# Order of one store, one load and eight residual adds around the second output group of a fused matmul, bias and residual kernel

## The chip, the cores and the metric

The kernel runs on one core of one Trainium2 chip. A core has a matrix engine (TensorE, called PE in the profile, with its weight loads as PEld), a vector engine (VectorE, DVE), a scalar engine (ScalarE, ACT), a general engine (GpSimd, POOL) and a queue processor (SyncE, SP) that here issues nearly all transfers between HBM and the on-chip memory. The transfers are carried out by 16 DMA engines. The metric is the device time of one execution in microseconds. "Before" is the kernel ahead of the change, "after" the kernel with it.

## The reference

```python
batch, m, k, n = 16, 512, 1024, 768
return (np.matmul(x, weight) + bias + residual).astype(np.float32)
```

All inputs and the output are float32. With the batch flattened there are 8192 rows: x is 8192 x 1024, the weight 1024 x 768, the bias has 768 numbers, residual and output are 8192 x 768. The page of the profile counts 61.88 MB read from HBM and 25.17 MB written.

## The kernel before, in words

The 8192 rows are worked on as 64 subtiles of 128 rows, t = 0 to 63, in 8 groups g of 8 subtiles (`G = 8`). A transfer moves a whole group: an x group is 4 MiB, a residual group 3 MiB, an output group 3 MiB. Only the first group of x and the weight are loaded in smaller pieces, and only the last output group is stored in pieces.

One subtile goes through the engines like this:

- `cast_x` (L121): ScalarE casts 128 x 1024 of x to bf16. There are five buffers for the result.
- `transpose` (L136): TensorE transposes it in eight 128 x 128 blocks into PSUM (two buffers).
- `copy_xt` (L143): VectorE copies the transposed block from PSUM to the on-chip memory (four buffers).
- `matmul` (L150): TensorE multiplies, 8 steps of k by 2 chunks of columns (512 and 256), into a PSUM tile of 128 x 768 (three buffers).
- `evacuate`: for groups 1 to 7, VectorE adds the PSUM tile to the residual tile, in place (L167), and GpSimd adds the bias, in place, afterwards (`add_bias`, L174). Group 0 is different: its residual isn't there yet, so VectorE adds bias to the PSUM tile and writes into a separate `o_tile` (L164), and the residual is added later, by GpSimd (`add_residual`, L178).

In the main loop, iteration t issues `cast_x(t + 3)`, the transposes of t + 1, the matmuls of t, `copy_xt(t + 1)` and `evacuate(t)`. Every instruction is recorded with `keep_in_program_order`, so each engine carries out its own instructions in the order in which the loop writes them. There is no scheduler. An engine whose next instruction has to wait holds everything behind it. This goes for the queue of SP too: a load that waits for a buffer holds the stores and loads written after it.

The residual groups, the staged weight and `o_tile` share four slots of 3 MiB, called ring0 to ring3. `HOME = [3, 1, 0, 3, 1, 2, 0, 3]` gives the slot of each residual group. Group 3's residual therefore goes where group 0's was: `load_r(3)` may not be issued until all eight `add_residual` have read group 0's residual. Group 4's goes where group 1's output was, so `load_r(4)` waits until `store(1)` has landed. Group 5's goes where `o_tile` was (`store(0)`). A store of a group waits for the bias adds of its eight subtiles.

The table `moves` gives the iterations at whose end SP's loads and stores are written. Around the change it says: the load of x group 3 and that of residual group 3 at t = 12, the store of group 1 at t = 15, the load of x group 4 at t = 20, the load of residual group 4 and the store of group 0 at t = 21, the load of x group 5 at t = 28. The eight residual adds are written at the end of t = 12, so on GpSimd they come ahead of the bias adds of subtiles 13, 14 and 15, for which `store(1)` waits.

At the end, the bias of subtiles 61 to 63 is added on VectorE ahead of time (t = 57 to 59), and group 7 is stored in five pieces of falling size, the last of which needs the last VectorE add (L293).

Of the kernel before, what the change touches and what calls it, by code (L numbers as in the profile page):

```python
# [11 lines left out]
G = 8  # L12
# [9 lines left out]
def kernel(  # L22
# [8 lines left out]
    nc = tc.nc  # L31
# [27 lines left out]
    def o(ins):  # L59
        return tc.keep_in_program_order(ins)  # L60
# [26 lines left out]
    x_tiles, r_tiles, o_tiles, w_stage = {}, {}, {}, {}  # L87
# [23 lines left out]
    def cast_x(t, split=False):  # L111
        if t >= n_sub:
            return
        xb_tiles[t] = slot(xb_pool, "xb", XB_BUFS, [P, K], BF16)
        src = x_tiles[t // G][:, t % G, :]
        if split:
            h = K // 2
            o(nc.scalar.copy(out=xb_tiles[t][:, :h], in_=src[:, :h]))  # L118
            o(nc.vector.tensor_copy(out=xb_tiles[t][:, h:], in_=src[:, h:]))  # L119
        else:  # L120
            o(nc.scalar.copy(out=xb_tiles[t], in_=src))  # L121
# [7 lines left out]
    def transpose(t):  # L129
        if t >= n_sub:  # L130
            return
        xb = xb_tiles.pop(t).rearrange("m (h p j) -> m h j p", p=P, j=4)
        pt = slot(pt_pool, "pt", PT_BUFS, [P, n_k, P], BF16)
        for k in range(n_k):
            h, j = divmod(k, 4)
            o(nc.tensor.transpose(out=pt[:, k, :], in_=xb[:, h, j, :], identity=ident))  # L136
        pt_tiles[t] = pt

    def copy_xt(t):
        if t >= n_sub:  # L140
            return
        xt_tiles[t] = slot(xt_pool, "xt", XT_BUFS, [P, n_k, P], BF16)
        o(nc.vector.tensor_copy(out=xt_tiles[t], in_=pt_tiles.pop(t)))  # L143

    def matmul(t, k0=0, k1=n_k):
        if t not in po_tiles:
            po_tiles[t] = slot(po_pool, "po", PO_BUFS, [P, N], FP32)
        for k in range(k0, k1):
            for (n0, nl) in chunks:
                o(nc.tensor.matmul(  # L150
                    po_tiles[t][:, n0:n0 + nl],
                    lhsT=xt_tiles[t][:, k, :],
                    rhs=w_sb[:, k, n0:n0 + nl],
                    start=(k == 0),
                    stop=(k == n_k - 1),
                ))

    def evacuate(t):


        g, j = divmod(t, G)
        po = po_tiles.pop(t)
        if g == 0:
            o(nc.vector.tensor_add(out=o_tiles[0][:, j, :], in0=po, in1=bias_bc))  # L164
        else:
            rt = r_tiles[g][:, j, :]
            o(nc.vector.tensor_add(out=rt, in0=po, in1=rt))  # L167
            if t < n_sub - 3:
                add_bias(t)
        xt_tiles.pop(t)  # L170

    def add_bias(t, engine=nc.gpsimd):
        rt = r_tiles[t // G][:, t % G, :]
        o(engine.tensor_add(out=rt, in0=rt, in1=bias_bc))  # L174

    def add_residual(t):
        ot = o_tiles[0][:, t, :]
        o(nc.gpsimd.tensor_add(out=ot, in0=ot, in1=r_tiles[0][:, t, :]))  # L178


    load_x(0, 0, 2)
# [42 lines left out]
    for k in range(2, 6):  # L224
# [19 lines left out]
    moves = {  # L244
        4: [(load_x, 2)],
        5: [(load_r, 0), (load_r, 2)],
        12: [(load_x, 3), (load_r, 3)],
        15: [(store, 1)],
        20: [(load_x, 4)],
        21: [(load_r, 4), (store, 0)],  # L250
        28: [(load_x, 5)],
# [11 lines left out]
    for t in range(3, n_sub - 1):  # L263
        cast_x(t + 3)
        if t == 3:
            matmul(t, 0, 5)
            transpose(t + 1)
            matmul(t, 5, 8)
        elif t == G - 1:
            matmul(t)  # L270
            transpose(t + 1)
        else:
            transpose(t + 1)
            matmul(t)
        copy_xt(t + 1)
        if n_sub - 7 <= t < n_sub - 4:
            add_bias(t + 4, nc.vector)
        evacuate(t)
        if t == 12:
            for u in range(G):  # L280
                add_residual(u)
        for move, *what in moves.get(t, []):
            move(*what)


    t = n_sub - 1
# [36 lines left out]
```

## Time and profile before

| what | value |
|---|---|
| median of 3 runs | 213.15 us (212.84 to 213.54) |
| profiled execution, device time | 214.12 us |
| its span in the profile | 212.3 us |
| mean granted TensorE clock | 0.993 |
| PE busy | 199.6 us (94%) |
| DVE busy | 110.3 us (52%) |
| POOL busy | 111.0 us (52%) |
| ACT busy | 66.7 us (31%) |
| queue q1 of the DMA engines | 87.03 MB, 97.3% of 16 engines' span |

The busy times are sums over the span. PE's are to be read with care: matmuls are pipelined and their ends are modelled, so that a busy PE is not PE at its peak. The span is cut into 40 slices of 5.3 us in the page's second part, with one digit for each engine and slice (tenths of busy time) and, for the DMA engines, their share and what they moved in GB/s. The timeline gives start and length of instructions; a number in brackets behind one is how long its engine sat idle ahead of it, and whom it waited for. For SP it gives the moments at which transfers are issued; the time to landing of each is told separately.

### The profile page before, as it was taken

To read this page: it belongs to the slowest core of one execution; us is meant where nothing else is said; L and a number is where in the kernel's file an instruction comes from. 1 tells how busy PE (TensorE), PEld (TensorE's weight loads), DVE (VectorE), ACT (ScalarE), POOL (GpSimd) and SP (SyncE) were. 2 spreads that over 40 slices of the span, in tenths; PEclk is the share of its full clock that TensorE was granted. 3 is DMA by queue.
4 is the path that set the end of the run, shared out by engine and by line. 5 is a ranking of instruction groups with operands and counts; after the bars stand their busy time and mean duration, and the time that the engine had idled before them with its cause. 6 is when DMAs were issued, how large, how long until landed. Compare 5 with 4: busy or idle time off the path is not lost.

```text
span 212.3 us, 3674 instructions
## 1 busy us (share of the span) xinstructions
PE 199.6 (94%) x1560; PEld 133.8 (63%) x1590; DVE 110.3 (52%) x143; ACT 66.7 (31%) x69; POOL 111.0 (52%) x68
## 2 busy tenths in 40 slices
PE   7797999999999999999999999999999999999960
PEld 7554666666666666666666666666666666666630
DVE  0646645545526554455445544554455445599630
ACT  2634409407330172200931046300751019300000
POOL 2000000366499999995566556555655665563600
PEclk9999999999999999999999999999999999999997
DMA  6999999999999899999999999999999999999993
GB/s 234 405 420 435 482 411 423 448 404 417 435 420 468 324 347 392 448 420 432 431 440 445 411 425 415 445 428 418 440 440 443 401 445 429 423 426 438 408 413 120
DMA packets 5640, 87.28 MB, mean 411 GB/s; under 512 B 628, under 2 KB 756, under 8 KB 2296
## 3 DMA queue, kind: packets, MB, share of 16 engines
q1 hardware_dynamic: 5616, 87.03, 97.3%
q8 instruction: 12, 0.20, 0.4%
q14 instruction: 4, 0.03, 0.0%
q10 hardware_dynamic: 8, 0.01, 0.0%
HBM read 61.88 MB, written 25.17 MB: 410 GB/s over the span
## 4 chain that ended last, share of the span: by engine, by line
PE 87%; DMA 7%; issue 1%; DVE 1%; ACT 0%; SPq 0%; POOL 0%; POOLq 0%
PE po L150 73%; PE pt L136 13%; DMA x_tile<-in_x_dram 4%; DMA bias_rows<-in_bias_dram 3%; PE last_ps L290 1%; DVE xt L143 1%; ACT xb L118 0%; DVE r_tile L293 0%; SPq L97 0%; POOL ident masks.py:197 0%; POOL bias_rows L73 0%; POOLq L307 0%
## 5 line engine op out<-in xcount | busy, mean ns | idle before, releaser
L150 PE MATMUL po<-w_sb,xt 128*128 128x512 bf16 (+1 forms) x978 | 172.2, 324 | 3.2 <-DVE xt L143 1.5
L174 POOL TENSOR_TENSOR r_tile<-r_tile,bias_bc 128x768 f32<-128x768 f32 x53 | 95.5, 1816 | 85.1 <-DVE r_tile L167 85.0
L150 PEld LDWEIGHTS <-xt 128*128 128x128 bf16 x1008 | 95.8, 98 | 59.7 <-DVE xt L143 2.5
L121 ACT CAST xb<-x_tile 128x1024 bf16<-128x1024 f32 x62 | 61.6, 1043 | 109.6 <-DMA x_tile<-in_x_dram 80.1
L167 DVE TENSOR_TENSOR r_tile<-po,r_tile 128x768 f32<-128x768 f32 x55 | 52.6, 956 | 76.1 <-PE po L150 65.8
L143 DVE COPY xt<-pt 128x1024 bf16<-128x1024 bf16 x64 | 43.5, 680 | 3.9 <-PE pt L136 3.9
L136 PEld LDWEIGHTS <-xb 128*128 128x128 bf16 x512 | 35.2, 113 | 9.3 <-ACT xb L118 2.0
L136 PE MATMUL pt<-ident,xb 128*128 128x128 bf16 x512 | 39.0, 219 | 1.4 <-ACT xb L118 1.4
L178 POOL TENSOR_TENSOR o_tile<-o_tile,r_tile 128x768 f32<-128x768 f32 x8 | 14.2, 1820 | 3.1 <-DMA r_tile<-in_residual_dram 3.1
L164 DVE TENSOR_TENSOR o_tile<-po,bias_bc 128x768 f32<-128x768 f32 x8 | 7.5, 952 | 4.8 <-PE po L150 4.8
L174 DVE TENSOR_TENSOR r_tile<-r_tile,bias_bc 128x768 f32<-128x768 f32 x3 | 6.6, 2188 | 0.0
L202 PE MATMUL warm_ps<-warm_in 128*128 128x128 bf16 x54 | 5.1, 275 | 1.1 <-DVE warm L76 1.1
L202 PEld LDWEIGHTS <-warm_in 128*128 128x128 bf16 x54 | 4.7, 129 | 1.0 <-DVE warm L76 1.0
L119 DVE CAST xb<-x_tile 128x512 bf16<-128x512 f32 x2 | 0.9, 426 | 6.3 <-DMA x_tile<-in_x_dram 6.3
L127 DVE CAST w_sb<-w_stage 128x768 bf16<-128x768 f32 x5 | 2.8, 558 | 2.5 <-DMA w_stage<-in_weight_dram 2.5
L125 ACT CAST w_sb<-w_stage 128x768 bf16<-128x768 f32 x3 | 2.5, 831 | 4.0 <-DMA w_stage<-in_weight_dram 4.0
L290 PE MATMUL last_ps<-w_sb,xt 128*128 128x512 bf16 (+1 forms) x16 | 2.8, 326 | 0.0
L290 PEld LDWEIGHTS <-xt 128*128 128x128 bf16 x16 | 1.6, 98 | 1.1
L118 ACT CAST xb<-x_tile 128x512 bf16<-128x512 f32 x2 | 1.2, 618 | 3.0 <-DMA x_tile<-in_x_dram 3.0
L77 ACT ACT_TABLE_LOAD x1 | 1.3, 1283 | 2.6 <-POOL ident masks.py:199 2.6
L293 DVE TENSOR_TENSOR r_tile<-last_ps,r_tile 128x512 f32<-128x512 f32 (+1 forms) x2 | 1.1, 558 | 1.0 <-PE last_ps L290 1.0
L228 DVE STREAM_SHUFFLE bias_bc<-bias_rows 128x768 f32<-128x768 f32 x1 | 1.0, 1012 | 0.0
(11 smaller groups left out, 2.1 us busy)
## 6 DMA issues: line engine op xcount, KB each, us to landing
x_tile<-in_x_dram SPq DMA_DIRECT2D x7, 4096.0 KB, 33.0
r_tile<-in_residual_dram SPq DMA_DIRECT2D x8, 3072.0 KB, 17.0
out_dram<-r_tile SPq DMA_DIRECT2D x6, 3072.0 KB, 23.9
x_tile<-in_x_dram SPq DMA_DIRECT2D x3, 1024.0 KB, 11.6
out_dram<-o_tile SPq DMA_DIRECT2D x1, 3072.0 KB, 23.9
w_stage<-in_weight_dram SPq DMA_DIRECT2D x6, 384.0 KB, 7.2
out_dram<-r_tile SPq DMA_DIRECT2D x1, 1536.0 KB, 9.7
x_tile<-in_x_dram SPq DMA_DIRECT2D x2, 512.0 KB, 7.9
```

Source lines behind the costliest of these rows:

```text
L121: o(nc.scalar.copy(out=xb_tiles[t], in_=src))
L125: o(nc.scalar.copy(out=w_sb[:, k, :], in_=w_stage[0][:, k, :]))
L127: o(nc.vector.tensor_copy(out=w_sb[:, k, :], in_=w_stage[0][:, k, :]))
L136: o(nc.tensor.transpose(out=pt[:, k, :], in_=xb[:, h, j, :], identity=ident))
L143: o(nc.vector.tensor_copy(out=xt_tiles[t], in_=pt_tiles.pop(t)))
L150: o(nc.tensor.matmul(po_tiles[t][:, n0:n0 + nl], lhsT=xt_tiles[t][:, k, :], rhs=w_sb[:, k, n0:n0 + nl], start=(k == 0), stop=(k == n_k - 1),))
L164: o(nc.vector.tensor_add(out=o_tiles[0][:, j, :], in0=po, in1=bias_bc))
L167: o(nc.vector.tensor_add(out=rt, in0=po, in1=rt))
L174: o(engine.tensor_add(out=rt, in0=rt, in1=bias_bc))
L178: o(nc.gpsimd.tensor_add(out=ot, in0=ot, in1=r_tiles[0][:, t, :]))
L202: o(nc.tensor.matmul(warm_ps, lhsT=warm_in, rhs=warm_in, start=True, stop=True))
L290: o(nc.tensor.matmul(ps, lhsT=xt_tiles[t][:, k, :], rhs=w_sb[:, k, n0:n0 + nl], start=(k == 0), stop=(k == n_k - 1)))
```

## The change

Three things are rearranged; no arithmetic is added or left out.

- On SP's queue, `load_r(3)` is moved from the end of t = 12 to the end of t = 17. `store(1)`, at t = 15, now stands ahead of it. Both stand between the load of x group 3 and that of x group 4, as before.
- On GpSimd, the residual adds are written at the end of t = 15 (`2 * G - 1`) in place of t = 12, behind the bias adds of all of group 1.
- Two of the eight residual adds, those of subtiles 0 and 1, go to VectorE, at t = 16 and t = 17, each between `copy_xt(t + 1)` and `evacuate(t)`. GpSimd keeps six.

```diff
-    def add_residual(t):
+    def add_residual(t, engine=nc.gpsimd):
         ot = o_tiles[0][:, t, :]
-        o(nc.gpsimd.tensor_add(out=ot, in0=ot, in1=r_tiles[0][:, t, :]))
+        o(engine.tensor_add(out=ot, in0=ot, in1=r_tiles[0][:, t, :]))
...
-        12: [(load_x, 3), (load_r, 3)],
+        12: [(load_x, 3)],
         15: [(store, 1)],
+        17: [(load_r, 3)],
         20: [(load_x, 4)],
...
             add_bias(t + 4, nc.vector)
+        if t in (2 * G, 2 * G + 1):
+            add_residual(t - 2 * G, nc.vector)
         evacuate(t)
-        if t == 12:
-            for u in range(G):
+        if t == 2 * G - 1:
+            for u in range(2, G):
                 add_residual(u)
```

## The prediction

> **What bounds the kernel now.** I read the page first: the slices, and the chain that ended last.
>
> ```profile
> PE   7797999999999999999999999999999999999960
> ...
> DMA  6999999999999899999999999999999999999993
> GB/s 234 405 420 435 482 411 423 448 404 417 435 420 468 324 347 392 448 420 432 431 440 445 411 425 415 445 428 418 440 440 443 401 445 429 423 426 438 408 413 120
> ...
> PE 87%; DMA 7%; issue 1%; DVE 1%; ACT 0%; SPq 0%; POOL 0%; POOLq 0%
> ```
>
> The chain says PE. But the DMA engines are just as full, and the only slices below 400 GB/s between the ramp and the end are the 14th to 16th (69 to 85 us). So two resources run neck and neck, and I ask which one ends last. The windows of the end, with those of the dip (columns: PE, PEld, DVE, ACT, POOL busy, clock, DMA share, GB/s):
>
> ```profile
> 69.00:71.50 2.50, 2.45 (x17) 1.49 (x16) 1.19 (x2) 0.00 (x0) 2.50 (x2) 1.00 0.67 288
> 71.50:73.50 2.00, 2.00 (x20) 1.36 (x18) 1.55 (x2) 0.14 (x1) 2.00 (x2) 1.00 1.09 340
> ...
> 76.50:80.50 4.00, 4.00 (x31) 2.60 (x30) 1.55 (x2) 1.80 (x2) 4.00 (x3) 1.00 1.00 283
> 80.50:92.00 11.50, 11.39 (x91) 7.70 (x92) 6.22 (x8) 3.14 (x3) 11.50 (x8) 1.00 1.01 434
> 184.00:198.00 14.00, 13.89 (x112) 9.34 (x112) 13.54 (x13) 1.04 (x1) 7.42 (x5) 1.00 1.01 430
> 198.00:206.00 8.00, 7.20 (x49) 4.37 (x48) 3.83 (x6) 0.00 (x0) 1.81 (x2) 1.00 0.97 410
> 206.00:209.00 3.00, 0.00 (x0) 0.00 (x0) 0.00 (x0) 0.00 (x0) 0.00 (x0) 1.00 0.79 314
> ```
>
> The compute ends at 205.71 (last L293 add: start 205.29, 0.42 long), yet the DMA engines move data at nearly full rate until 209. The last store, 128 KB, is issued at 205.74 and lands 5.7 us later, at 211.4. How long would it take with an empty queue? Nearest row: the first x load (1 MiB, issued at 0.74) landed in 4.7 us, of which 2.4 is its bytes at 430 GB/s; an estimate of 2.3 + 0.1 = 2.4. So a landing at 208.1 is what PE allows, and 3.3 us of the end is backlog of the DMA queue. From 80.5 to 209 that queue never runs dry (430 GB/s throughout), so a microsecond lost at 70 to 80 us is still there at 211.4.
>
> How much was lost: ScalarE's first cast of each x group starts when that group has landed.
>
> ```profile
> 49.04 3.89 ACT L121 CAST xb<-x_tile 128x1024 bf16<-128x1024 f32 x4 [9.33 <-DMA x_tile<-in_x_dram]
> ...
> 73.36 3.89 ACT L121 CAST xb<-x_tile 128x1024 bf16<-128x1024 f32 x4 [9.28 <-DMA x_tile<-in_x_dram]
> ...
> 100.92 5.82 ACT L121 CAST xb<-x_tile 128x1024 bf16<-128x1024 f32 x6 [12.46 <-DMA x_tile<-in_x_dram]
> ...
> 125.19 5.93 ACT L121 CAST xb<-x_tile 128x1024 bf16<-128x1024 f32 x6 [12.35 <-DMA x_tile<-in_x_dram]
> ```
>
> Between two of these always 10 MiB pass. The gaps are 24.3, 27.6, 24.3, and then 24.9 and 24.2 (landings at 150.09 and 174.33). The second is 3.1 longer than the mean of the others, 24.4. By the windows, against 430 GB/s: 2.5 x (1 - 288/430) + 2.0 x (1 - 340/430) = 1.25 ahead of 73.5, and 4.0 x (1 - 283/430) = 1.37 from 76.5 to 80.5, 2.6 in all as a mean over the engines. And why there:
>
> ```profile
> 39.74 0.33 SPq L92 DMA_DIRECT2D x_tile<-in_x_dram  x1
> 70.58 0.33 SPq L102 DMA_DIRECT2D r_tile<-in_residual_dram  x1
> 75.91 0.35 SPq L106 DMA_DIRECT2D out_dram<-r_tile  x1
> 76.35 0.38 SPq L92 DMA_DIRECT2D x_tile<-in_x_dram  x1
> ```
>
> ```profile
> SPq L102 <- POOL o_tile L178: 14.3, 1, 14.3
> ```
>
> SP issued nothing from 40.07 to 70.58: `load_r(3)` stood behind GpSimd's eight residual adds (start 56.31, 14.24 long), when x group 3, the last thing queued, was all but through (landed 73.3).
>
> **The change, part by part.** *SP.* `store(1)` no longer stands behind `load_r(3)`. It needs the bias of subtile 15: its L167 starts at 59.49, GpSimd follows an L167 by 1.03 (185.50 after 184.46) and takes 1.81, so 62.3, and it is issued at 62.4 instead of 75.91, 11 us ahead of x group 3's landing. It fills the DMA queue to 73.3 + 7.3 = 80.6 (3 MiB at 430 GB/s). `load_r(3)` follows when the six GpSimd adds are done: 62.3 + 6 x 1.78 = 73.0, plus up to two waits of 0.8 for VectorE (below), so 73.0 to 74.7. Later than 70.58, but 6 us ahead of its turn. The load of x group 4 (needs the cast of subtile 23, over at 64.08) goes out at 75, ahead of 76.35. Nothing else passes anything: `load_r(4)` waits for `store(1)` landed (80.6, was 91.14).
>
> I take it that the dip is gone whole: 2.6 (mean engine) to 3.1 (slowest, by which landings go). I take 2.8. Ends: nothing saved, if the slow stretch returns on other packets, to 3.3, where PE stops it.
>
> *GpSimd.* Same adds, two fewer; its bias adds of group 1 come sooner, those of group 2 start at 73 to 75, before at 75.9 (70.51 + 3 x 1.79). Hidden.
>
> *VectorE.* Two adds more, at the one spot where it has been late:
>
> ```profile
> 64.13 0.96 DVE L167 TENSOR_TENSOR r_tile<-po,r_tile 128x768 f32<-128x768 f32 x1 [3.08 <-ACT xb L121]
> 65.00 0.68 DVE L143 COPY xt<-pt 128x1024 bf16<-128x1024 bf16 x1
> 65.60 0.94 DVE L167 TENSOR_TENSOR r_tile<-po,r_tile 128x768 f32<-128x768 f32 x1
> ```
>
> Subtile 16's L167 comes 1.6 late (62.54 would be the beat of 3.05 us); I put that down to residual group 2. What an add costs beside GpSimd:
>
> ```profile
> 185.94 2.19 DVE L174 TENSOR_TENSOR r_tile<-r_tile,bias_bc 128x768 f32<-128x768 f32 x1
> 188.05 0.94 DVE L167 TENSOR_TENSOR r_tile<-po,r_tile 128x768 f32<-128x768 f32 x1
> ```
>
> GpSimd's add ran from 185.50 to 187.31; VectorE's ended 0.82 after it. The other two pairs (ends 190.88 and 191.70, 194.46 and 195.28) give 0.82 too: such an add waits for GpSimd's running add, then takes 0.82. Add 0: from 60.97, GpSimd's bias add ends at 62.3, done at 63.1, ahead of 64.13. Free. Add 1: from 65.60; GpSimd's adds, pushed by 0.8, end at 64.95 and 66.75, so 67.6; then L167 (0.87 to the next start) and the copy for subtile 19 (0.68) to 69.1, where its matmuls were to start at 68.88. PE is held 0.25, between 0 (no wait) and 0.9 (a full GpSimd add). PE has no idle time later to make it up.
>
> The Trainium skill, "SBUF — State Buffer", section "Who interferes with whom", says that a VectorE instruction with two SBUF inputs and a GpSimd instruction that reads SBUF exclude each other for the whole instruction, the first to issue holding the port. That agrees with the 0.82 rows, but it doesn't say who is next when GpSimd has adds queued; each instruction in turn gives 210.4, GpSimd keeping the port gives 219.9 (third rival).
>
> *Residual group 3* lands at 73.3 + 7.3 + 7.3 = 87.9. Subtile 24's L167 is due at 59.49 + 9 x 3.05 = 86.9, plus 0.25. It comes 0.7 late; being 1.6 late at subtile 16 cost PE nothing. Hidden; the cover is gone at 1.7 late.
>
> *Sum.* Landing: 211.4 - 2.8 = 208.6, with PE's limit at 208.1 + 0.25 = 208.35 below it. Span 212.3 - 2.8 = 209.5; profiled time 214.12 - 2.8 = 211.3. That execution lies 0.97 above the median, so I subtract from the median: 213.15 - 2.8 = 210.35, say 210.4.
>
> **The rivals.**
> 1. *Half of the dip returns.* The stretch 76.5 to 80.5 begins 0.6 after the store and the x load were issued, with r group 3 still under way, and isn't explained by an empty queue. If issuing close ahead of the end does it, `load_r(3)` and x group 4 at 74 to 75 do it again: gain 1.25, time 211.9. Against it: the piece of group 7 issued at 198.07, with 6 us queued, brought nothing of the kind (410 GB/s).
> 2. *VectorE loses two GpSimd adds for each of its own*, 1.8 more each: the copies come late by 2.9 in all, PE allows 208.1 + 2.9 = 211.0, gain 0.4: 212.7.
> 3. *Slower: GpSimd's queued adds shut VectorE out.* Add 0 waits till 73.0, done 73.8; L167 and the copy for subtile 18 follow by 75.4, needed at 65.83: PE stands 9.6, and 0.5 more after add 1. Landing 208.1 + 10.1 = 218.2, 6.8 later: 219.9. It decides from 3.3 us of PE stall on. No row of before shows VectorE facing a second queued GpSimd add: the three pairs each had GpSimd idle 1.76 afterwards.
> 4. *No change*, because PE bounds, as the chain has it: 213.15. Against it: DMA running to 209.
>
> **How the numbers follow.** Forecast 0.50 (209.7 to 211.2), first rival 0.22, second 0.11, third 0.12, fourth 0.05. About 0.3% (0.64 us) is what a measurement can tell from no change. Faster: 0.50 + 0.22 + 0.05 (half of the second); same: 0.06 of the second and 0.02 of the fourth; slower: the third and 0.03 of the fourth. The range 209.7 to 212.9 leaves out the third rival and the rest.
>
> **What would show it.** Right: store at 62.4 and `load_r(3)` at 73 to 75 on SP; no slice below 400 GB/s around 75; x group 4 landing near 98 instead of 100.9; the last store's time to landing down from 5.7 towards 3. Wrong: L178 on VectorE far above 2.2 us, L150 waiting for L143 by microseconds at 65 to 75, or the low GB/s reappearing elsewhere.

## The result and the profile after

After takes 211.29 us (median of 4 runs, 211.06 to 211.38) beside 213.34 us for before in the same session; the ratio is 0.9900, 95% interval 0.9869 to 0.9931. On another chip, with after and before side by side once more, it was 211.19 against 213.70, ratio 0.9875 (0.9842 to 0.9907). So 2.0 to 2.5 us are gained; 2.8 were forecast. The profiled execution took 211.21 us, its span 209.4. Of all runs in this document one, of before, took 305.83 us at a granted clock of 0.659 and is left out of every median and ratio.

The page of after, first the slices and then the chain that ended last:

```profile
PE   7797999999999999999999999999999999999992
...
DMA  6999999999999999999999999999999999999895
GB/s 232 402 424 440 448 404 444 419 451 413 418 468 430 410 418 430 443 432 419 427 437 432 426 421 440 444 426 427 413 441 448 426 421 407 437 443 432 355 403 222
...
PE 88%; DMA 7%; issue 1%; DVE 1%; ACT 0%; SPq 0%; POOL 0%; POOLq 0%
```

The shares of the chain read as they did for before. What changed stands in the DMA rows: the dip of the 14th to 16th slices is gone, and the first slice below 400 GB/s is now the third from the end, where the DMA engines have little left but the stores of group 7, which PE is still producing. The windows that the prediction showed of before, now of after (columns: PE, PEld, DVE, ACT, POOL busy, clock, DMA share, GB/s):

```profile
69.00:71.50 2.50, 2.45 (x20) 1.58 (x19) 1.57 (x3) 0.00 (x0) 2.50 (x3) 1.00 0.96 410
71.50:73.50 2.00, 2.00 (x20) 1.38 (x18) 1.52 (x2) 0.00 (x0) 2.00 (x2) 1.00 0.92 393
...
76.50:80.50 4.00, 4.00 (x31) 2.58 (x31) 1.63 (x3) 2.12 (x3) 4.00 (x3) 1.00 1.05 446
...
206.00:209.00 3.00, 0.00 (x0) 0.00 (x0) 0.01 (x1) 0.00 (x0) 0.00 (x0) 1.00 0.45 167
```

288, 340 and 283 GB/s have become 410, 393 and 446. After 206 only 167 GB/s are moved instead of 314: the backlog of the end has shrunk. ScalarE's first casts show the same time coming back:

```profile
49.07 3.89 ACT L121 CAST xb<-x_tile 128x1024 bf16<-128x1024 f32 x4 [9.13 <-DMA x_tile<-in_x_dram]
...
73.68 3.89 ACT L121 CAST xb<-x_tile 128x1024 bf16<-128x1024 f32 x4 [9.37 <-DMA x_tile<-in_x_dram]
...
97.94 3.89 ACT L121 CAST xb<-x_tile 128x1024 bf16<-128x1024 f32 x4 [9.19 <-DMA x_tile<-in_x_dram]
```

From x group 3 to x group 4 it is now 24.3 us instead of 27.6. SP's queue, and the landing of the very last store (a 128 KB piece, issued at 206.03):

```profile
62.60 0.35 SPq L106 DMA_DIRECT2D out_dram<-r_tile  x1
74.67 0.33 SPq L102 DMA_DIRECT2D r_tile<-in_residual_dram  x1
75.09 0.78 SPq L92 DMA_DIRECT2D x_tile<-in_x_dram  x1
80.90 0.33 SPq L102 DMA_DIRECT2D r_tile<-in_residual_dram  x1
```

```profile
out_dram<-r_tile SPq DMA_DIRECT2D x1, 128.0 KB, 2.5
```

The store left at 62.60, the load at 74.67, 6.2 us ahead of the moment (80.90) at which `load_r(4)` saw that store landed. The last store landed 2.5 us after its issue instead of 5.7.

### The profile page after: what moved, and what is told of

The parts are those of the page before. It is cut to its first block, busy times and chain, and to the rows that moved or that the text cites. A ratio compares the mean times of both kernels' runs of the same rounds, so it can differ in the third digit from the quotient of the medians.

```text
span 209.4 us, 3673 instructions
## 1 busy us (share of the span) xinstructions
PE 199.8 (95%) x1560; PEld 134.1 (64%) x1590; DVE 113.9 (54%) x145; ACT 67.2 (32%) x69; POOL 109.1 (52%) x66
## 4 chain that ended last, share of the span: by engine, by line
PE 88%; DMA 7%; issue 1%; DVE 1%; ACT 0%; SPq 0%; POOL 0%; POOLq 0%
PE po L150 74%; PE pt L136 13%; DMA x_tile<-in_x_dram 5%; DMA bias_rows<-in_bias_dram 3%; PE last_ps L293 1%; DVE xt L143 1%; ACT xb L118 0%; DVE r_tile L296 0%; SPq L97 0%; POOL ident masks.py:197 0%; POOL bias_rows L73 0%; POOLq L310 0%
## 5 line engine op out<-in xcount | busy, mean ns | idle before, releaser
L167 DVE TENSOR_TENSOR r_tile<-po,r_tile 128x768 f32<-128x768 f32 x55 | 52.6, 956 | 72.5 <-PE po L150 65.0
L178 POOL TENSOR_TENSOR o_tile<-o_tile,r_tile 128x768 f32<-128x768 f32 x6 | 12.1, 2056 | 0.0
L164 DVE TENSOR_TENSOR o_tile<-po,bias_bc 128x768 f32<-128x768 f32 x8 | 7.5, 953 | 4.8 <-PE po L150 4.8
L178 DVE TENSOR_TENSOR o_tile<-o_tile,r_tile 128x768 f32<-128x768 f32 x2 | 3.9, 1944 | 0.0
L293 PE MATMUL last_ps<-w_sb,xt 128*128 128x512 bf16 (+1 forms) x16 | 2.8, 326 | 0.0
L293 PEld LDWEIGHTS <-xt 128*128 128x128 bf16 x16 | 1.6, 98 | 1.1
```

The costliest lines, as they stand in the source:

```text
L178: o(engine.tensor_add(out=ot, in0=ot, in1=r_tiles[0][:, t, :]))
L293: o(nc.tensor.matmul(ps, lhsT=xt_tiles[t][:, k, :], rhs=w_sb[:, k, n0:n0 + nl], start=(k == 0), stop=(k == n_k - 1)))
```

## The experiments

Each experiment was timed beside before on its own chip.

### Before once more: is the second half of the dip chance?

No edit.

> The kernel before, unchanged, for a second profile. All theories: 213.3 us. What it tells apart: the loss at 69 to 85 us had two parts, a start with an empty queue (69 to 73.5, 1.25 us against 430 GB/s) and a slow stretch at 76.5 to 80.5 (283 GB/s, 1.37 us), which begins just after the store of group 1 and the load of x group 4 are issued. If the second part belongs to the order of the queue, it comes back at the same place (under 320 GB/s from 76.5 to 80.5); if it was a chance event of one execution, that stretch shows 420 GB/s or more and the landings of x groups 2 and 3 lie about 26 us apart instead of 27.6.

Measured: 214.01 against 213.93 us, ratio 1.0005 (0.9983 to 1.0026), as it must be. The slices of this second profile of before:

```profile
GB/s 231 406 421 425 484 412 433 435 416 396 444 424 473 313 352 396 443 426 426 435 426 441 416 440 410 453 438 412 430 430 430 444 423 419 423 440 429 409 411 114
```

313, 352 and 396 stand where the first profile had 324, 347 and 392, and x groups 3 and 4 are 27.6 us apart again (73.48, 101.10). From 76.5 to 80.5 this execution moved 301 GB/s, under the 320 that were named. So neither half of the dip is the chance of one execution. That both belong to the order of the queue is shown by after, which has another order and neither half.

### Does the DMA queue set the end?

Before, and then after, with half of the store of group 0 left out (the same line is edited in both); PE's work is the same. This half of the output is not written.

```diff
-        21: [(load_r, 4), (store, 0)],
+        21: [(load_r, 4), (store, 0, 0, 4)],
```

> Before, with the store of group 0 cut to its first four subtiles (1.5 MiB are not written, 3.65 us of queue time at 430 GB/s); all else the same, PE's work untouched. This part of the output is left out. My theory (the DMA queue sets the end, PE's own limit lies 3.0 to 3.3 lower): 3.0 faster, 210.3 us. Rival, PE is the bound as the chain has it: no change, 213.3.

> After, with the same half of the store of group 0 left out. My theory: after is within 0.9 us of PE's limit (last store issued at 206.03, landing 2.5 later instead of about 1.7 with an empty queue), so it gains 0.4 to 0.9 only: 210.4 to 210.9 us, the same as before with the half store. Rival, the queue still sets the end of after by more: 209 or less. Rival, PE is the bound of both: no change, 211.3.

Measured: before with the half store 211.12 us, ratio 0.9872 to before (0.9833 to 0.9911), 2.5 faster, though not one instruction of PE, VectorE or GpSimd was removed. After with the half store 211.14, ratio 0.9879 to before (0.9845 to 0.9913): by the medians hardly faster than after itself (211.19 to 211.29), where I had expected 0.4 to 0.9. So the queue set the end of before, against the chain's 87% for PE, and both kernels come to the same floor near 211.1. That the floor is PE's is read from the last store: in both profiles it now lands 1.8 us after its issue, behind no backlog.

```profile
out_dram<-r_tile SPq DMA_DIRECT2D x1, 128.0 KB, 1.8
```

In after it took 2.5, so after stands within 0.7 us of the floor, not quite on it: two of the six runs with the half store took 210.4, the profiled one among them, though its last add starts only 0.06 earlier than in after (205.52 and 205.58). Nor is the floor one fixed number. In the profile of before with the half store the last add starts at 206.24 instead of 205.29, because PE's first subtiles came 0.95 later. A window of after with the half store:

```profile
196.00:199.00 3.00, 3.00 (x26) 1.99 (x24) 2.44 (x4) 0.00 (x0) 2.54 (x2) 1.00 0.00 0
```

With an estimated 3.65 us of transfers less (1.5 MiB at 430 GB/s), the DMA engines stand still ahead of the stores of group 7 (0 GB/s), and the median hardly moves. That is what a queue off the critical path looks like; in the same window after moves 328 GB/s and before 434.

### One part alone: the order on SP's queue

```diff
-        12: [(load_x, 3), (load_r, 3)],
+        12: [(load_x, 3)],
         15: [(store, 1)],
+        17: [(load_r, 3)],
```

> Before, with only the queue order of the change: the store of group 1 ahead of the load of residual group 3, all eight residual adds on GpSimd at t = 12 as before. My theory (the end is set by the DMA queue, and what counts is that it never runs dry): the store still waits for GpSimd until 75.9, the queue is empty from 73.3 to about 77, residual group 3 lands near 92 and VectorE and PE wait for it some 3.5 us. The loss on the queue is about 4.2 in place of 3.1, so 1.1 slower than before: 214.4 us. Rival, the order of the two transfers alone brings the gain: 211.3. Rival, PE is the bound and its stall adds in full: 216.8.

Measured: 218.46 us, ratio 1.0197 (1.0168 to 1.0225), 4.5 slower. The store waited for GpSimd until 76.28, as expected, and residual group 3 came later than I had reckoned. VectorE and PE in that profile:

```profile
94.69 0.96 DVE L167 TENSOR_TENSOR r_tile<-po,r_tile 128x768 f32<-128x768 f32 x1 [8.90 <-DMA r_tile<-in_residual_dram]
```

```profile
96.31 5.30 PE L150 MATMUL po<-w_sb,xt 128*128 128x512 bf16 x16 [5.57 <-DVE xt L143]
```

VectorE waits 8.90 us for the residual, the copy for the next subtile stands behind it, and PE is idle for 5.57. Then one subtile's matmuls take 5.30 instead of 2.76. The windows say why (the number ahead of the DMA share is the granted clock):

```profile
90.00:92.00 2.00, 0.74 (x10) 0.56 (x8) 0.00 (x0) 0.00 (x0) 0.45 (x1) 1.00 1.14 492
92.00:94.00 2.00, 0.00 (x0) 0.00 (x0) 0.00 (x0) 0.00 (x0) 0.00 (x0) 1.00 0.91 389
94.00:96.00 2.00, 0.00 (x0) 0.00 (x0) 1.31 (x2) 0.00 (x0) 0.27 (x1) 0.77 1.02 442
96.00:98.00 2.00, 1.70 (x6) 0.75 (x7) 1.71 (x3) 0.00 (x0) 2.00 (x2) 0.50 1.18 508
98.00:100.00 2.00, 2.00 (x8) 0.99 (x7) 0.00 (x0) 0.00 (x0) 1.30 (x1) 0.50 0.83 360
```

The idle PE is given half its clock, and keeps it until about 102. Idle and half clock together move the last VectorE add (L293 of before) from 205.29 to 214.13, 8.8 us. The last store then lands 1.8 us after its issue, so PE, not the queue, ends this kernel. The two lie close, though: the queue lost 6.3 us between x groups 3 and 4 here and 1.5 more between 4 and 5. None of the three lines that I had written down held: the swap alone brings no gain, the loss is far over 1.1, and PE's stall isn't added in full to the time of before. The swap needs the bias adds ahead of the residual adds.

### The other part alone: the order on GpSimd

```diff
-        12: [(load_x, 3), (load_r, 3)],
-        15: [(store, 1)],
+        12: [(load_x, 3)],
+        15: [(load_r, 3), (store, 1)],
...
-        if t == 12:
+        if t == 2 * G - 1:
             for u in range(G):
                 add_residual(u)
```

> Before, with only the order on GpSimd of the change: residual adds (all eight, on GpSimd) behind the bias adds of group 1, the load of residual group 3 still ahead of the store of group 1. My theory: the load waits until 76.8, the store that could have gone at 62.6 stands behind it, the DMA queue is empty from 73.3 to about 77.8 (about 5.1 lost with the slow start, against 3.1 before): 2.0 slower, 215.3 us, with PE never held (residual group 3 lands near 86). Rival, PE is the bound: no change, 213.3.

Measured: 218.68 us, ratio 1.0226 (1.0205 to 1.0247), 4.8 slower. The sign and the place are as expected, the size isn't. Windows of this profile:

```profile
71.00:73.00 2.00, 2.00 (x19) 1.39 (x18) 1.08 (x2) 0.00 (x0) 2.00 (x2) 1.00 0.16 66
73.00:75.00 2.00, 2.00 (x17) 1.32 (x16) 0.51 (x2) 1.58 (x2) 2.00 (x3) 1.00 0.00 0
75.00:77.00 2.00, 1.95 (x17) 1.29 (x16) 1.52 (x2) 2.00 (x3) 2.00 (x2) 1.00 0.00 0
77.00:79.00 2.00, 2.00 (x19) 1.43 (x18) 0.99 (x2) 0.80 (x2) 2.00 (x2) 1.00 0.81 205
79.00:81.00 2.00, 2.00 (x16) 1.24 (x15) 0.57 (x1) 0.56 (x1) 2.00 (x2) 1.00 0.86 369
81.00:83.00 2.00, 1.95 (x19) 1.35 (x18) 1.55 (x2) 1.04 (x1) 2.00 (x2) 1.00 1.00 430
83.00:85.00 2.00, 2.00 (x19) 1.37 (x18) 0.90 (x2) 0.39 (x1) 2.00 (x2) 1.00 1.17 381
85.00:87.00 2.00, 2.00 (x15) 1.23 (x13) 0.66 (x2) 0.65 (x1) 2.00 (x2) 1.00 0.88 233
```

Three things are to be seen. Most of the DMA engines are done with x group 3 two microseconds ahead of its landing, which is that of the slowest one (66 GB/s from 71 to 73). Then nothing moves at all until the load issued at 76.80 begins. And the slow stretch of before comes back as well: full rate at 81 to 83, then 381 and 233 at the tail of residual group 3, just ahead of the store. The first casts of x groups 3 and 4 are 32.4 us apart (73.42, 105.80): 8.0 lost, where I had reckoned 5.1. PE computes through these windows (1.95 to 2.00 of 2.00). It is held later, for 1.51 us at 105.4, where it waits for x group 4 itself, and its last add starts at 208.24 instead of 205.29. The last store lands 7.3 us after its issue instead of 5.7, so the queue ends this kernel, and by more than it ended before.

### How early must the load be? VectorE's two adds

After once more, with all eight adds on GpSimd at the end of t = 15:

```diff
-        if t in (2 * G, 2 * G + 1):
-            add_residual(t - 2 * G, nc.vector)
...
-            for u in range(2, G):
+            for u in range(G):
```

> After, with all eight residual adds on GpSimd (none on VectorE). My theory: the load of residual group 3 is issued at 76.8 instead of 74.7, still 1.6 us ahead of the first DMA engine's running dry and 3.6 ahead of the last; the time stays at 211.3, within 0.4. Rival, the two VectorE adds are what makes the load early enough, or an issue this close ahead brings the slow stretch back: 212.3 or more. Rival, the VectorE adds cost PE something: below 211.0.

Measured: 212.43 us, ratio to before 0.9933 (0.9908 to 0.9958). That is 1.1 above after's first result, so the 211.3 that I had expected was wrong. But it was on another chip, and in that profile PE's early part ran 1.2 us late (the last L164 add starts at 36.64, in after at 35.44). So it was run again beside after, together with a kernel that keeps all eight adds on GpSimd but puts two of them into gaps:

```diff
-        if t in (2 * G, 2 * G + 1):
-            add_residual(t - 2 * G, nc.vector)
...
+        if t in (2 * G - 3, 2 * G - 2):
+            add_residual(t - 2 * G + 3)
         if t == 2 * G - 1:
             for u in range(2, G):
```

> After, unchanged, on the same chip as the next two. 0.9900 of before, 2.0 to 2.2 us faster.

> After, with all eight residual adds on GpSimd, once more, beside after itself. In its first profile the load of residual group 3 was issued at 78.8, the engines had run dry (341 GB/s), and the first subtiles had come 1.3 us later than in after. If the issue time of that load is what counts: 0.6 to 1.5 us slower than after, with a slice under 400 GB/s near 80 us. If the first result was that one execution: within 0.3 us of after.

> After, with all eight residual adds on GpSimd, but those of subtiles 0 and 1 placed behind the bias adds of subtiles 13 and 14, in gaps of 1.23 us that GpSimd has there. The store of group 1 goes out near 63.8 (62.6 in after), the load of residual group 3 near 74.6 (74.7 in after), and VectorE has no residual add. If the issue time of the load is what counts: the same as after within 0.3 us. If the VectorE adds do something else: like the kernel with all eight adds at the end of t = 15. If the VectorE adds cost PE anything: up to 0.3 us faster than after.

Measured, on one chip: after 211.19 us; all eight at t = 15: 212.39, ratio to before 0.9933 (0.9906 to 0.9959); two in the gaps: 211.37, ratio to before 0.9888 (0.9859 to 0.9916). SP's issue of `load_r(3)` and of the load that follows `store(1)`'s landing, with all eight at t = 15:

```profile
76.76 0.33 SPq L102 DMA_DIRECT2D r_tile<-in_residual_dram  x1
77.18 0.40 SPq L92 DMA_DIRECT2D x_tile<-in_x_dram  x1
80.62 0.33 SPq L102 DMA_DIRECT2D r_tile<-in_residual_dram  x1
```

and with two in the gaps:

```profile
75.18 0.33 SPq L102 DMA_DIRECT2D r_tile<-in_residual_dram  x1
75.60 0.64 SPq L92 DMA_DIRECT2D x_tile<-in_x_dram  x1
80.96 0.33 SPq L102 DMA_DIRECT2D r_tile<-in_residual_dram  x1
```

By lead I mean how far ahead of the end of the transfer in front a load is issued. 3.9 us of lead costs 1.2 us of time, 5.8 costs nothing that can be told. The VectorE adds matter because they bring the load forward; without them, but with the load at nearly the same time, after's time is kept within 0.2 us. In the kernel with 3.9 us of lead the price isn't even paid there. From 76.5 to 80.5 it moves 428 GB/s; the loss comes at 100 to 105, at the tail of residual group 4 ahead of `store(0)`:

```profile
100.00:105.00 5.00, 4.95 (x37) 3.20 (x36) 2.42 (x4) 2.62 (x3) 3.42 (x2) 1.00 0.98 359
```

After has 428 there.

### The empty queue in another place

After, with the six GpSimd adds three subtiles later:

```diff
-        17: [(load_r, 3)],
+        18: [(load_r, 3)],
...
-        if t == 2 * G - 1:
+        if t == 2 * G + 2:
             for u in range(2, G):
```

> After, with the six GpSimd residual adds moved three subtiles later (end of t = 18), so that the load of residual group 3 is issued near 82.9, when the store of group 1 has landed (80.4): the empty queue comes back in another place, with the queue order of after. My theory: about 4.1 us lost on the queue, PE held about 3.0 for residual group 3; the queue ends last: 4.0 slower than after, 215.3 us. Rival, only PE's stall counts: 3.0 slower than after, 214.3. Rival, the order store ahead of load is what counts: 211.3. If a slow stretch (under 350 GB/s) shows again 5 to 8 us after the restart, it belongs to a restart; if not, to what was issued in before at that time.

Measured: 218.54 us against 213.60, ratio 1.0230 (1.0188 to 1.0272), 7.3 above after where I expected 4.0. The load was issued at 83.03 and nothing moved from 80 to 82. PE stood 3.96 us for residual group 3, then worked at half clock (4.30 for a subtile's matmuls); the last add starts at 211.41 instead of 205.58. The last store lands 3.5 us after its issue, against 1.8 without a backlog, so the queue ends this kernel, as expected, but it lost about 8.0 (5.1 between x groups 3 and 4, 2.9 between 4 and 5) where I had reckoned 4.1. The order store ahead of load, which this kernel has, saved nothing. And the second slow stretch isn't 5 to 8 us behind the restart but 20 behind it, at 105 to 110, again at the tail of residual group 4 ahead of `store(0)`:

```profile
84.00:86.00 2.00, 2.00 (x19) 1.44 (x18) 1.55 (x2) 1.05 (x1) 2.00 (x2) 1.00 1.09 332
...
105.00:110.00 5.00, 5.00 (x43) 3.37 (x42) 3.11 (x4) 2.81 (x3) 2.53 (x3) 1.00 1.02 344
```

### All together

The loss is the gap between two x groups' first casts, less 24.4. The lead, again, is the end of the transfer in front (x group 3's cast, or `load_r(4)`'s issue) less the issue of the first transfer behind it.

| kernel | lead, us | lost on the queue, us | time, us |
|---|---|---|---|
| after, first profile | 6.2 | 0 (x 3 to 4) | 211.3 |
| all on GpSimd, two in gaps | 5.8 | 0 (x 3 to 4) | 211.4 |
| all on GpSimd, second run | 3.9 | 1.4 (x 4 to 5) | 212.4 |
| before | 2.8 | 3.2 (x 3 to 4) | 213.3 to 213.9 |
| all on GpSimd, first run | 1.9 | 1.9 (x 3 to 4), 1.5 (x 4 to 5) | 212.4, profiled 214.4 |
| SP's order alone (PE ends last) | -2.6 | 6.3 (x 3 to 4), 1.5 (x 4 to 5) | 218.5 |
| GpSimd's order alone | -3.4 | 8.0 (x 3 to 4) | 218.7 |
| after, adds three subtiles later | under 0 | 5.1 (x 3 to 4), 2.9 (x 4 to 5) | 218.5 |

Where nothing is lost, the time lies 0.2 to 0.3 us above the floor of 211.1. Where something is lost, it lies above the floor by the loss less 0.1 to 1.0 us; for the first run of all adds on GpSimd this holds for the profiled execution, from which its losses are read.

## Why the prediction was right, and where its size was off

*What ends last.* Right, and now shown: take transfers away and before falls to 211.1; take them from after and the median hardly moves. The rival "no change, because PE bounds" falls with that. The chain named PE since it follows waits back from the last instruction, and that one waits for PE; the queue behind the last store isn't in it.

*The moved steps.* Store at 62.60 (62.4 forecast), load at 74.67 (73.0 to 74.7), x group 4's load at 75.09 (75), `load_r(4)` at 80.90 (80.6).

*VectorE's adds.* They took 2.19 and 1.70 us. The timeline of VectorE, then the group of L178 on GpSimd (durations in ns, least, median and most), both of after:

```profile
61.19 2.19 DVE L178 TENSOR_TENSOR o_tile<-o_tile,r_tile 128x768 f32<-128x768 f32 x1
64.47 0.96 DVE L167 TENSOR_TENSOR r_tile<-po,r_tile 128x768 f32<-128x768 f32 x1 [1.09 <-ACT xb L121]
65.35 0.68 DVE L143 COPY xt<-pt 128x1024 bf16<-128x1024 bf16 x1
65.94 1.70 DVE L178 TENSOR_TENSOR o_tile<-o_tile,r_tile 128x768 f32<-128x768 f32 x1
67.57 0.94 DVE L167 TENSOR_TENSOR r_tile<-po,r_tile 128x768 f32<-128x768 f32 x1
```

```profile
L178 POOL TENSOR_TENSOR o_tile<-o_tile,r_tile x6: 1812/1821/2537, 62.5 to 72.8; 128x768 f32<-128x768 f32 x6
```

The first ended at 63.38, 0.81 behind GpSimd's bias add (60.76, 1.81 long), although six more adds were queued there; the second was through in 1.70; and a GpSimd add was stretched from 1.82 to as much as 2.54. In these rows the two engines take turns, one add each. The rivals in which VectorE loses two turns, or all, are refuted for this queue of six adds. The first L167 after the new add was late as in before; that it waited for residual group 2 was only argued, there and here. What the adds cost PE: the last add starts at 205.58 instead of 205.29, and the whole kernel ran 0.23 later from the first L164 on (17.64 against 17.41), which leaves 0.06; forecast 0.25. In the second profile of after the same difference is 0.32. It arises at the matmuls of subtile 17, ahead of the second new add, behind an L167 of subtile 16 at 64.53; the kernel with two adds in gaps and none on VectorE has that L167 as late (64.52), so the 0.32 can't be put down to the new adds.

*Residual group 3's cover.* Subtile 24's L167 came at 88.25, 1.0 late where 0.7 was forecast, and PE wasn't held. With the residual still later the cover is gone, as the two kernels with PE idle for 5.57 and 3.96 us show.

*The first rival,* the slow stretch coming back because of issues close ahead of the end: not in after (446 GB/s), but it was near. With 3.9 us of lead instead of 6.2 it takes 1.2 us.

*The sum.* The landing was right: 208.6 forecast, 206.03 + 2.5 = 208.5 measured. Worked against the profiled execution, 214.12 - 2.8 = 211.3, and after's profiled execution took 211.21. The step that failed is the last one. The same 2.8 was then taken from the median, 0.97 lower, "That execution lies 0.97 above the median, so I subtract from the median". But after doesn't lie a fixed distance under before: it lies within 0.7 us of PE's floor. By that floor a run of before that took 213.15 had only some 2 to lose. After's runs lie within 0.3 us of each other, those of before spread over more than one, which fits; but no faster run of before was profiled, so this reading of the spread is argued, not shown. The measured 211.29 is 0.9 above the forecast of 210.4, just outside the band of 209.7 to 211.2 that was given one half, and below the 211.9 of the first rival.

The bound was in the text, as a landing at 208.1 that PE allows; it should have been a bound on the time. Its own term was mis-sized too: 128 KB at 430 GB/s are 0.3 us, not 0.1, so the estimate of an empty queue's landing should have read 2.6, and the half-store kernels measured 1.8. By that figure PE allowed 207.5 in the profiled execution of before.

## What to carry to other kernels

When an engine and the DMA queue are both near 100% busy, ask which one is still working behind the last compute instruction; half a store left out tests it. In a queue that ends last and never runs dry any gap is paid at the end, so look for the transfer that makes the queue wait, and put one that is ready in front of it; but the one in front must truly be ready: the swap without the reordered adds cost 4.5 us. Price a gain down to the next floor, not from the median by a fixed amount.

## What the runs showed of the hardware that I had not expected

- A queue that runs low can cost more than its gap. In all kernels with a lead under 4 us, eight profiles of six kernels, the DMA engines lost time (with 3.9 us of lead only there, otherwise a second time) at the tail of a residual load just ahead of a store: at 76.5 to 80.5 in before (283 GB/s), at 100 to 105 with 3.9 us of lead (359), at 105 to 110 in the kernel with the late adds (344). The DMA share in these three stretches is 0.98 to 1.02: the engines were busy, and moved less. In the four profiles with a lead of 5.8 us or more the stretch wasn't there (428 GB/s from 100 to 105 in after); the two kernels with all adds on GpSimd differ in the times of issue, the lead above all, and not in the order of loads and stores. In the kernel with only SP's order changed it came as late as 108 to 110 (246 GB/s), some 30 us behind the gap. Why a low queue should be paid for that much later stays open.
- A residual for which VectorE waits 8.90 us costs PE twice: 5.57 us idle, then half clock (0.50) until about 102. The Trainium skill, "TensorE: Matmul & The Clock Gate", section "Part 1: The HAM clock gate (the "warmup" mystery)", has the array fall to half its clock after at least one idle window of about 3.4 us and come back after at least one such window of sustained work. Idle times of 5.57 and 3.96 us did the first here: the clock fell 4.3 and 3.7 us after PE's last work, which agrees. It came back 5.5 and 3.1 us after the work began again; the 3.1 is a little under the page's figure.
